# Both 512-token parts of a recurrence head in one step, turned outputs, advance splits of pooling maps, and wider tiles for branch A's gates: one decoder layer on Trainium2

## Chip, cores and metric

The kernel runs on one core of one Trainium2 chip. The metric is the device time of one execution, in microseconds (us); lower is better.

## The reference, cut to what matters

One layer of a decoder trunk for 1024 tokens of width 1024, all in float32:

```python
x = x + 0.5 * swiglu_1(rms(x))                        # D_FF = 2816
h = rms(x); proj = h @ w_in                           # 1024 x 6656, columns q, f, i, og, pool, gate A, gate B
# A: 8 heads, a state of 128 x 128 per head
f = lb + (1 - lb) * sigmoid(f)
S_t = diag(f_t) S_{t-1} + outer(1 - f_t, i_t)
o_t = S_t^T silu(q_t)                                 # RMS norm per head, times silu(og), then @ w_branch_a
# B: trailing means over 2, 4, 8, 16 tokens minus the token, a 128 x 128 map per group,
#    a scale per channel, then @ w_branch_b
y = sigmoid(gate_A) * y_A + sigmoid(gate_B) * y_B
x = x + y @ w_out
x = x + 0.5 * swiglu_2(rms(x))
x = x + sigmoid(rms(x) @ w_gate) * rms(p @ w_ple)
return rms(x)
```

## The kernel before

**Products.** Every big product is cut into 2 x 2 blocks and computed by a scheme of seven block products instead of eight (`SIDES`). Each float32 operand is split into a high part (ScalarE's cast, L118) and a low part (VectorE's subtraction, L119), and a product is three matmuls, high x high, high x low, low x high, of 128x128 by 128x512 (`mm3`, L157 to L159). Three such matmuls are called a triple here. `pair` computes two column blocks of a projection: it yields once per triple, 28 times (`PAIR`), and the last products are deferred into the next pair. Sums of weight blocks are GpSimd's (L90, L93).

**Stages.** The first feed-forward part runs from 0 to about 715 us. The projections by `w_in` and, between them, the recurrence run from about 775 to 1450. Then come the rest of branch B's product with `w_branch_b` (`branch_b`) and the loading of the recurrence's outputs (`load_act`), to 1485; branch A's product with `w_branch_a`, whose results are gated and added to branch B's (to about 1570); the product with `w_out`; the second feed-forward part; the embedding's gate; and the final norm, to 2415.

**The recurrence.** `hgrn(h, half)` computes one of the two 512-token halves of a head without a loop over tokens. Its tiles are `qk` (q and k side by side, 128x1024), `f`, `tot` (products of f over 2, 4, 8 ... tokens), `v` and `og`. The diagonal of the score matrix comes from a product of k and q (L925, copied under a mask at L927). Seven levels follow (`LEVELS`, hh = 1 to 64): four small matmuls (L954), float32 by float32, which are eight passes; then the copy of their result into the scores, under a mask on VectorE (L958) for hh < 32 and by ScalarE (L966) from 32 on; then one VectorE multiply of q and k by the products of f (L974, through the helper `mul`, L87), which the next level's matmuls read. After the levels k is transposed (L981, copied at L983), k times v (L986) gives the state updates (L998, L1000), and the scores and the state give the outputs (L1009, L1011). The norm follows: four squares on ScalarE (L1015), `rstd` on VectorE (L168) and GpSimd (L169), and a VectorE multiply (L1017). `turn` transposes the result (L1025), multiplies by the gate (L1026) and stores it. The transposes of `v` (L933) stand ahead of the levels.

**Order.** TensorE's order is as the program writes it (`tc.manual_schedule`). `hgrn` yields 13 times per half, and `head` runs half 0 and then half 1, 26 steps per head (`GROUPS`). At each step `among` puts some triples of the head's three `pair` generators behind the small matmuls: 84 triples per head, 74 in head 7, 4 more in heads 0 and 2 for the pooling maps. `turn` of a half is issued at step 2 of the next half, and the last one after the loop. For the other engines and for SyncE, which issues all DMAs (`load`, L149; `store`, L153), a scheduler sets the order at build time; each engine's queue is then worked through in order.

**Memory.** PSUM has three banks for `pA`, one each for `pB` and `pC`, and three for `aux`, which all small matmuls, transposes and pooling maps share. In SBUF a tile takes a buffer of its tag: "q" has four of 1024 columns, "h" five of 512, "w" twelve of 1024, "a" 28 of 1024, "u" eight of 512. `v`, `og`, `tot`, `ga` and `yb` use "h"; `qk` uses "q", and so do four of the `x` tiles of the product with `w_out`.

**Pooling maps.** `pool_maps` runs as one of the generators of heads 0 and 2: two groups by two halves, and for each a split (`hilo_half`, L118 and L119) followed at once by the triple that reads it, the scale and the store. The trailing means that a map reads are VectorE work spread beside an earlier pair (`beside_means`).

**Branch A.** For each of 32 results `done` loads 512 columns of `ga` and of `yb` into two "h" tiles, multiplies (L87), adds (L84) and stores.

Of the kernel before, what the change touches and what calls it, by code (L numbers as in the profile page):

```python
# [13 lines left out]
AF = mybir.ActivationFunctionType  # L14
# [23 lines left out]
def hybrid_block(ctx: ExitStack, tc: tile.TileContext, a: dict, out: bass.AP):  # L38
# [47 lines left out]
    def mul(o, x, y):  # L86
        nc.vector.tensor_tensor(o, x, y, ALU.mult)  # L87
# [672 lines left out]
    def qf_pair(h):  # L760
        qk, f = [t_("q", "qk") for _ in range(2)], [t_("u", "f") for _ in range(2)]
        heads[h] = qk, f

        def q_(half):
            def go(q):
                k = qk[half][:, R]
                nc.scalar.activation(k, q, AF.Sigmoid)
                mul(q, q, k)
            return go

        def f_(half):
            def go(src):
                nc.scalar.activation(f[half], src, AF.Sigmoid)
                nc.vector.tensor_scalar(
                    f[half], f[half], lb1[:, h : h + 1], lb[:, h : h + 1], ALU.mult, ALU.add
                )
            return go
# [87 lines left out]
    def pool_maps():  # L865

        r = t_("h", "pwr")
        load(r.rearrange("p (g d) -> p g d", g=NG), a["pool_w"].rearrange("g c d -> c g d"))
        wh, wl = hilo_half(r, "w", "pwhl")
        while pooled:  # L870
            g, u = pooled.pop(0)
            gc = slice(g * P, (g + 1) * P)
            for half in range(2):
                ph, pl = hilo_half(u[half], "w", "pb")
                ps = bank("aux")
                mm3(ps, wh[:, gc], wl[:, gc], ph, pl, True, True)
                nc.scalar.mul(u[half], ps, pscale[:, g : g + 1])
                store(m_dram[g][half], u[half])
                yield False
# [14 lines left out]
    v_next = []  # L894

    def v_load(h, half):
        assert (h, half) in v_there
        return load(t_("h", "v"), v_dram[h][half], True)

    def v_of(h, half):  # L900
        return v_next.pop() if v_next else v_load(h, half)


    states = {}

# [3 lines left out]
    def hgrn(h, half):  # L909
# [8 lines left out]
        state = states.get(h)  # L918
# [7 lines left out]
        yield  # L926
# [4 lines left out]
        ps = bank("aux")  # L931
        for p_, v_ in zip(chunks(ps), chunks(v)):
            nc.tensor.transpose(p_, v_, ident)  # L933
        yield
        nc.scalar.copy(v, ps)
        vc = chunks(v)
# [3 lines left out]
        at = 0  # L940
        for hh in LEVELS:
            n = HALF // (2 * hh)
            pv = tots[hh].rearrange("p (a two) -> p a two", two=2)
            tots[2 * hh] = tot[:, at : at + n]
            mul(tots[2 * hh], pv[:, :, 0], pv[:, :, 1])
            at += n
        mul(q, q, f)
        for hh in LEVELS:
# [6 lines left out]
            yield  # L955
# [15 lines left out]
            na = HALF // (2 * hh)  # L971
            both = view(qk, hh, [[HALF - hh, 2], [2 * hh, na], [1, hh]])
            by = view(tots[hh], 0, [[1, 2], [2, na], [0, hh]])
            mul(both, both, by)  # L974

        need = 4 - half
        ps = bank("aux")
        for p_, a_ in zip(chunks(ps)[:need], kc):  # L980
            nc.tensor.transpose(p_, a_, ident)  # L981
        yield
        nc.scalar.copy(k[:, : need * P], ps[:, : need * P])  # L983
# [3 lines left out]
        yield  # L987
        assert (h, half) in og_there
        og = load(t_("h", "og"), og_dram[h][half], True)
        og_last[0] = latest[0]  # L990
        befores = []

        for c, (s_, p_) in enumerate(zip(chunks(f), chunks(ps))):
# [5 lines left out]
            else:  # L999
                nc.vector.scalar_tensor_tensor(  # L1000
                    s_, state, tots[128][:, c : c + 1], p_, ALU.mult, ALU.add
                )
            state = s_
        states[h] = state

# [6 lines left out]
        yield  # L1012
# [19 lines left out]
    GROUPS = 2 * 13  # L1032
    turns = []

    def head(h):

        for half in range(2):
            for i, _ in enumerate(hgrn(h, half)):
                if i == 2 and turns:
                    turns.pop(0)()  # L1040
                if i == 7:
                    at = 2 * h + half + 1
                    if at < 2 * HEADS:
                        v_next.append(v_load(at // 2, at % 2))
                yield
# [342 lines left out]
```

## Time and profile before

| | us |
|---|---|
| median of 3 runs (2415.89 to 2421.88) | 2416.18 |
| the profiled execution | 2417.04 |
| its span in the trace | 2415.3 |
| TensorE matmul busy | 2330.6 |
| TensorE weight load busy (beside the matmuls) | 1916.1 |
| VectorE busy | 1471.4 |
| ScalarE busy | 980.0 |
| GpSimd busy | 444.8 |

The DMAs moved 331.75 MB, 137 GB/s over the span. In the rows of the profile PE is TensorE, PEld its weight loads, DVE VectorE, ACT ScalarE, POOL GpSimd, SP or SPq SyncE's queue. A row of the timeline has the start and the duration in us, the engine, the line of the kernel, the operation, the tile written and the tiles read (buffer numbers left out), and the shape; a bracket at its end says how long the engine idled just before it and for whom. A row of waits has the sum, the number and the longest, in us. A row of the stretches has the window and its length, then for PE, PEld, DVE, ACT and POOL the busy time and the number of instructions, then the granted TensorE clock, the share of time in which the DMA engines were busy, and GB/s; where the view was asked for one engine alone, only that engine's busy time stands there. A row of groups has busy time and mean ns of one, then the engine's idle time before them. Busy matmuls overlap a little in the trace, so a matmul's price is read from start to start.

### The profile page before, as it was taken

What the parts mean: (1) busy time and instruction counts of PE and PEld (TensorE: products, weight loads), DVE (VectorE), ACT (ScalarE), POOL (GpSimd) and SP (SyncE); (2) the same over time, 40 slices, a digit from 0 to 9 for tenths busy, and PEclk for the clock granted to TensorE, in tenths of its full rate; (3) what the DMA queues carried; (4) which work ended last, traced back from release to release, by engine and by line L of the source; (5) the groups of instructions that cost most, each with busy time, mean ns of one, the idle gap of its engine ahead of it and who ended that gap; (6) DMA issues with size and microseconds to landing.
All of it is one profiled execution on the core that took longest, in us unless ns stands there. A gap on an engine that the chain in (4) does not pass through costs nothing. (4 is left out here: it accounts for less than half of the span.)

```text
span 2415.3 us, 29471 instructions
## 1 busy us (share of the span) xinstructions
PE 2330.6 (96%) x11058; PEld 1916.1 (79%) x11058; DVE 1471.4 (61%) x2037; ACT 980.0 (41%) x1528; POOL 444.8 (18%) x397
## 2 busy tenths in 40 slices
PE   8999999999998999999999999999899999999997
PEld 6778888888877888788888877877687888888886
DVE  6555554567656766766566566676544544568568
ACT  6344333333554333333333343237333333334556
POOL 1332223200011222122222102102222222100000
PEclk9999999999999999999999999999999999999999
DMA  4344453484332232222222257652234533663334
GB/s 183 127 143 168 156 174 132 153 322 128 117 114 70 79 96 83 75 88 79 83 81 86 88 189 247 229 207 105 87 129 146 177 102 110 215 251 127 97 100 152
DMA packets 133759, 331.75 MB, mean 137 GB/s; under 512 B 15216, under 2 KB 16240, under 8 KB 133616
## 3 DMA queue, kind: packets, MB, share of 16 engines
q1 hardware_dynamic: 133616, 329.87, 40.1%
q8 instruction: 87, 1.43, 0.3%
q14 instruction: 56, 0.46, 0.1%
HBM read 228.62 MB, written 101.19 MB: 137 GB/s over the span
## 5 line engine op out<-in xcount | busy, mean ns | idle before, releaser
L90 POOL TENSOR_TENSOR s<-rb 128x512 f32<-128x512 f32 x74 | 98.5, 1331 | 780.1 <-DMA rb<-in_ffn_w_dram 352.6
L119 DVE TENSOR_TENSOR wtl<-rb,wth 128x1024 fp32r<-128x1024 f32 x74 | 90.7, 1225 | 152.7 <-ACT wth L118 152.7
L118 ACT CAST wsh<-s 128x1024 fp32r<-128x1024 f32 x74 | 77.8, 1052 | 229.6 <-POOL s L93 215.5
L119 DVE TENSOR_TENSOR wsl<-s,wsh 128x1024 fp32r<-128x1024 f32 x74 | 91.3, 1233 | 117.9 <-ACT wsh L118 117.9
L93 POOL TENSOR_TENSOR rb<-ra,s 128x512 f32<-128x512 f32 x74 | 96.7, 1306 | 349.0 <-DVE wd L119 335.6
L118 ACT CAST wth<-rb 128x1024 fp32r<-128x1024 f32 x74 | 77.7, 1049 | 183.8 <-POOL rb L93 183.8
L954 PEld LDWEIGHTS aux<-qk 128*128 128x128 f32 (+1 forms) x896 | 109.7, 186 | 37.9 <-issue 11.5
L118 ACT CAST gh<-gr 128x1024 fp32r<-128x1024 f32 x84 | 81.8, 980 | 141.8 <-PE aux L158 86.4
L119 DVE TENSOR_TENSOR wal<-ra,wah 128x1024 fp32r<-128x1024 f32 x74 | 91.5, 1238 | 75.1 <-PE pC L158 45.0
L119 DVE TENSOR_TENSOR gl<-gr,gh 128x1024 fp32r<-128x1024 f32 x84 | 95.0, 1134 | 68.2 <-ACT gh L118 68.1
L157 PE MATMUL pA<-xT3h,wth 128*128 128x512 f32 x296 | 119.7, 404 | 8.9 <-ACT g L382 6.8
L954 PE MATMUL aux<-qk 128*128 128x64 f32 (+1 forms) x896 | 110.5, 267 | 17.2 <-DVE qk L87 11.5
L118 ACT CAST wah<-ra 128x1024 fp32r<-128x1024 f32 x74 | 77.6, 1050 | 117.6 <-DMA ra<-in_ffn_w_dram 97.2
L157 PE MATMUL pA<-xT1h,wsh 128*128 128x512 f32 x280 | 114.1, 408 | 10.4 <-ACT xT1h L118 7.1
L157 PE MATMUL pB<-xT1h,wsh 128*128 128x512 f32 x296 | 119.3, 403 | 2.6 <-DVE g L81 1.3
L157 PE MATMUL pA<-x0h,wah 128*128 128x512 f32 x296 | 118.5, 400 | 1.2 <-DVE gb L87 0.7
L157 PE MATMUL pC<-x0h,wah 128*128 128x512 f32 x296 | 118.9, 402 | 0.0
L157 PE MATMUL pB<-x,wth 128*128 128x512 f32 x296 | 118.8, 401 | 0.0
L158 PE MATMUL pA<-x0l,wah 128*128 128x512 f32 x296 | 115.8, 391 | 1.6 <-DVE x0l L119 1.6
L158 PE MATMUL pB<-xT1l,wsh 128*128 128x512 f32 x296 | 116.6, 394 | 0.8 <-DVE xT1l L119 0.8
L157 PE MATMUL pA<-xT3h,wd 128*128 128x512 f32 x280 | 112.8, 403 | 4.3 <-ACT c L385 2.5
L159 PE MATMUL pA<-xT3h,wtl 128*128 128x512 f32 x296 | 116.4, 393 | 0.5 <-DVE wtl L119 0.5
(341 smaller groups left out, 6602.1 us busy)
## 6 DMA issues: line engine op xcount, KB each, us to landing
ra<-in_ffn_w_dram SPq DMA_DIRECT2D x47, 512.0 KB, 3.7
rb<-in_ffn_w_dram SPq DMA_DIRECT2D x44, 512.0 KB, 3.7
gsS<-gs SPq DMA_DIRECT2D x88, 256.0 KB, 2.2
rB<-in_ffn_w_dram SPq DMA_DIRECT2D x40, 512.0 KB, 7.0
gr<-gsS SPq DMA_DIRECT2D x40, 512.0 KB, 3.4
gsA<-g SPq DMA_DIRECT2D x66, 256.0 KB, 2.0
gr<-gsA SPq DMA_DIRECT2D x30, 512.0 KB, 5.9
ra<-in_w_in_dram SPq DMA_DIRECT2D x27, 512.0 KB, 3.6
```

Source lines behind the costliest of these rows:

```text
L90: nc.gpsimd.tensor_tensor(o, x, y, ALU.add)
L93: nc.gpsimd.tensor_tensor(o, x, y, ALU.subtract)
L118: nc.scalar.copy(hi, src)
L119: nc.vector.tensor_tensor(lo, src, hi.bitcast(F32), ALU.subtract)
L157: nc.tensor.matmul(ps, ah, bh, start=first, stop=False, **kw)
L158: nc.tensor.matmul(ps, ah, bl, start=False, stop=False, **kw)
L159: nc.tensor.matmul(ps, al, bh, start=False, stop=last, **kw)
L954: nc.tensor.matmul(ps[:m, c, :64], kc[c][:, :m], right, start=True, stop=True)
```

## The change

It has three parts. Lines of the changed kernel lie some lower: L928 is the product of k and q, L944 the level matmuls, L952 the masked copy, L960 ScalarE's copies, L975 the transposes of `v`, L984 those of k, L992 k times v, L1001 and L1003 the state updates, L1013 and L1015 the outputs, L1020 the norm's multiply, L1028 and L1029 the turn.

1. **Recurrence.** The two halves of a head run side by side: one step holds the same step of half 0 and of half 1, and a head has 12 steps instead of 26. In a level the multiply now stands ahead of the masked copy. The products of f are made one per level instead of all at the start; the last ones go into a constant tile (`decays`, in the room of `lbr`). k = 1 - f is made when q and f are finished (`k_` in `qf_pair`). `v` is loaded at the third level (hh = 4) and transposed after the last level; `og` is loaded at the step of the k transposes. A head's two turns are issued at steps 1 and 2 of the next head, and those of head 7 one behind the other after the loop.
2. **Pooling maps.** The split of the next map is issued one part ahead of the map that reads it, the first one in a part of its own, so heads 0 and 2 have 5 more parts instead of 4.
3. **Branch A.** `ga` and `yb` are loaded into the halves of one 1024-column "q" tile instead of two "h" tiles.

```diff
@@ qf_pair
+        def k_(half):
+            if half in made:
+                nc.scalar.activation(qk[half][:, R], f[half], AF.Copy, scale=-1.0, bias=1.0)
+            made.add(half)
...
@@ pool_maps
-        while pooled:
-            g, u = pooled.pop(0)
+        todo = [(g, half, u[half]) for g, u in pooled for half in range(2)]
+        pooled.clear()
+        parts = [hilo_half(todo[0][2], "w", "pb")]
+        yield False
+        for i, (g, half, u) in enumerate(todo):
             gc = slice(g * P, (g + 1) * P)
-            for half in range(2):
-                ph, pl = hilo_half(u[half], "w", "pb")
-                ps = bank("aux")
-                mm3(ps, wh[:, gc], wl[:, gc], ph, pl, True, True)
...
+            if i + 1 < len(todo):
+                parts.append(hilo_half(todo[i + 1][2], "w", "pb"))
+            ps = bank("aux")
+            mm3(ps, wh[:, gc], wl[:, gc], *parts.pop(0), True, True)
...
@@ hgrn
-        nc.scalar.activation(k, f, AF.Copy, scale=-1.0, bias=1.0)
-        v = v_of(h, half)
+        yield
...
-        for hh in LEVELS:
-            n = HALF // (2 * hh)
-            pv = tots[hh].rearrange("p (a two) -> p a two", two=2)
-            tots[2 * hh] = tot[:, at : at + n]
-            mul(tots[2 * hh], pv[:, :, 0], pv[:, :, 1])
-            at += n
-        mul(q, q, f)
...
         for hh in LEVELS:
+            yield
...
                 nc.tensor.matmul(ps[:m, c, :64], kc[c][:, :m], right, start=True, stop=True)
-            yield
+            na = HALF // (2 * hh)
+            both = view(qk, hh, [[HALF - hh, 2], [2 * hh, na], [1, hh]])
+            by = view(tots[hh], 0, [[1, 2], [2, na], [0, hh]])
+            mul(both, both, by)
             if hh < 32:
...
-            mul(both, both, by)
+            at = HALF - HALF // hh
+            pv = tots[hh].rearrange("p (a two) -> p a two", two=2)
+            tots[2 * hh] = decays[half] if hh == 64 else tot[:, at : at + na]
+            mul(tots[2 * hh], pv[:, :, 0], pv[:, :, 1])
+            if hh == 4:
+                v = load(t_("h", "v"), v_dram[h][half], True)
...
-    GROUPS = 2 * 13
+    GROUPS = 12
...
@@ head
-        for half in range(2):
-            for i, _ in enumerate(hgrn(h, half)):
-                if i == 2 and turns:
-                    turns.pop(0)()
...
-                yield
+        two = [hgrn(h, half) for half in range(2)]
+        for it in two:
+            next(it)
+        for i in range(GROUPS):
+            for it in two:
+                next(it, None)
+            if i in (1, 2) and turns:
+                turns.pop(0)()
+            yield
...
-            among(its, head(h), (74 if h == 7 else 3 * PAIR + 4 * (h in (0, 2))))
-        turns.pop(0)()
+            among(its, head(h), (74 if h == 7 else 3 * PAIR + 5 * (h in (0, 2))))
+        while turns:
+            turns.pop(0)()
...
@@ branch A, done
-            ga = load(t_("h", "ga"), ga_dram[j + i][half])
-            yb = load(t_("h", "yb"), yb_dram[j + i][half])
+            both = t_("q", "gy")
+            ga = load(both[:, L], ga_dram[j + i][half])
+            yb = load(both[:, R], yb_dram[j + i][half])
```

The first place is VectorE's queue in a head, from the masked copy of the level hh = 2 to the multiply of the level hh = 8 (before); `score_5481` is half 0's score matrix and `score_5482` half 1's, `o` tiles are results of projections, and `wsl` and `wtl` low parts of weights.

```order
L958 COPY_PREDICATED score_5481<-mask_77,aux_8696 128x128x2
L87 TENSOR_TENSOR qk_8188<-qk_8188,tot_8660 128x2x128x2
L87 TENSOR_TENSOR qk_8602<-qk_8602 128x512
L87 TENSOR_TENSOR o_8409<-o_8409,pA_8434 128x512
L958 COPY_PREDICATED score_5481<-mask_81,aux_8715 128x64x4
L87 TENSOR_TENSOR qk_8188<-qk_8188,tot_8660 128x2x64x4
L81 TENSOR_TENSOR o_8407<-o_8407,pB_8530 128x512
L119 TENSOR_TENSOR wsl_8823<-s_1591_8819,wsh_8822 128x1024
L87 TENSOR_TENSOR o_8407<-o_8407,sg_8730 128x512
L958 COPY_PREDICATED score_5481<-mask_85,aux_8740 128x32x8
L87 TENSOR_TENSOR qk_8188<-qk_8188,tot_8660 128x2x32x8
```

The same place after:

```order
L1029 SCALAR_TENSOR_TENSOR og_8454<-aux_8723,onorm,og_8454 128x512
L81 TENSOR_TENSOR o_8391<-o_8391,pB_8512 128x512
L119 TENSOR_TENSOR wsl_8835<-s_1593_8831,wsh_8834 128x1024
L87 TENSOR_TENSOR o_8391<-o_8391,sg_8737 128x512
L87 TENSOR_TENSOR qk_8200<-qk_8200,tot_8596 128x2x64x4
L952 COPY_PREDICATED score_5481<-mask_81,aux_8758 128x64x4
L87 TENSOR_TENSOR qk_8201<-qk_8201,tot_8604 128x2x64x4
L952 COPY_PREDICATED score_5482<-mask_81,aux_8768 128x64x4
L119 TENSOR_TENSOR wd_8838<-rb_8829,wd_8838 128x512
L119 TENSOR_TENSOR wtl_8844<-rb_8829,wth_8843 128x1024
```

Before, each level is a masked copy and then the multiply that the next level waits for, with projection work between levels. Now a level is two such couples, multiply first, one per half, with the projection work (`wd`, `wtl`) behind both.

The second place is the end of head 7 on VectorE, from the last state updates of half 1 to the last turn; `gb` rows are branch B's gates, `b` rows and `x0l` the sums and splits of the recurrence's earlier outputs in `load_act`.

```order
L1000 SCALAR_TENSOR_TENSOR f_9835<-f_9835,tot_10796,aux_10949 128x128 x2
L84 TENSOR_TENSOR b_1925_11170<-b_1926_11171,b_1925_11170 128x512
L168 TENSOR_SCALAR rso_11001<-rso_11001 128x4
L87 TENSOR_TENSOR gb_10964<-yb_10966,gb_10964 128x512
L1017 TENSOR_TENSOR qk_9833<-aux_10978,rso_11001 128x512
L84 TENSOR_TENSOR b_1926_11171<-b_1926_11171 128x512
L87 TENSOR_TENSOR gb_10995<-yb_10997,gb_10995 128x512
L1026 SCALAR_TENSOR_TENSOR og_10973<-aux_11020,onorm,og_10973 128x512
```

After, for both halves:

```order
L1003 SCALAR_TENSOR_TENSOR f_9838<-f_9838,lbr,aux_10925 128x128 x2
L168 TENSOR_SCALAR rso_10969<-rso_10969 128x4
L1020 TENSOR_TENSOR qk_9835<-aux_10961,rso_10969 128x512
L119 TENSOR_TENSOR x0l_11177<-b_1925_11170,x0h_11176 128x1024
L168 TENSOR_SCALAR rso_10986<-rso_10986 128x4
L84 TENSOR_TENSOR b_1925_11170<-b_1926_11171,b_1925_11170 128x512
L1020 TENSOR_TENSOR qk_9836<-aux_10977,rso_10986 128x512
L87 TENSOR_TENSOR gb_10996<-yb_10998,gb_10996 128x512
L1029 SCALAR_TENSOR_TENSOR og_10883<-aux_11013,onorm,og_10883 128x512
L1029 SCALAR_TENSOR_TENSOR og_10890<-aux_11020,onorm,og_10890 128x512
```

Before, only half 1's norm (L168, L1017) stands here. Now the norms of both halves do, with `x0l` and an addition between them. On TensorE 18 matmuls of `branch_b` lay between the last output matmul and the turn; now 12 lie between the last output matmul and the two turns.

The third place is SyncE's queue: loads of `x` for the product with `w_out` (rows with `x_dram`), before among branch B's stores.

```order
L149 DMA x_12141<-x_dram_9_136 128x1024
L153 DMA yb_dram_0_151_278<-gb_11303 128x512
L149 DMA ra_11515<-in_w_branch_a_dram 128x1024
L153 DMA yb_dram_1_152_279<-gb_11320 128x512
L153 DMA yb_dram_0_153_280<-gb_11342 128x512
L149 DMA x_12150<-x_dram_10_137 128x1024
L153 DMA yb_dram_1_154_281<-gb_11359 128x512
L149 DMA rb_11521<-in_w_branch_a_dram 128x1024
L149 DMA x_12159<-x_dram_11_138 128x1024
L149 DMA x_12168<-x_dram_12_139 128x1024
```

After, the same loads:

```order
L149 DMA y_11994<-y_dram_0_157_284 128x512
L149 DMA y_11994<-y_dram_0_161_288 128x512
L149 DMA x_12125<-x_dram_9_136 128x1024
L149 DMA rB_2069_12001<-in_w_out_dram 128x1024
L149 DMA rB_2072_12007<-in_w_out_dram 128x1024
L149 DMA rB_2075_12013<-in_w_out_dram 128x1024
L153 DMA y_dram_1_170_297<-o_11801 128x512
L153 DMA y_dram_0_169_296<-o_11802 128x512
L149 DMA y_12019<-y_dram_0_163_290 128x512
L149 DMA y_12019<-y_dram_0_167_294 128x512
L149 DMA x_12134<-x_dram_10_137 128x1024
L149 DMA x_12143<-x_dram_11_138 128x1024
```

They have moved behind branch A, to where the product with `w_out` fetches `y` and its weights.

More of the change, by code (lines that the diff above doesn't have):

```diff
@@ L892, in pool_pair @@
         yield from out_pair(w_in[PU + g], w_in[PU + g + 1], act, done)
[L894 to L901, printed above, removed]
     states = {}
+    decays = [lbr[:, i, :4] for i in range(2)]
     def view(t, offset, dims):
@@ L969, in hgrn @@
                     )
[L971 to L974 removed]
+            at = HALF - HALF // hh
[3 more added lines that the diff above has]
+            if hh == 4:
+                assert (h, half) in v_there
+                v = load(t_("h", "v"), v_dram[h][half], True)
+        yield
+        ps = bank("aux")
+        for p_, v_ in zip(chunks(ps), chunks(v)):
+            nc.tensor.transpose(p_, v_, ident)
+        nc.scalar.copy(v, ps)
+        vc = chunks(v)
         need = 4 - half
+        yield
         ps = bank("aux")
```

38 lines of the change are left out of this document (15 added, 23 removed).

## The prediction

> **What bounds the kernel now.** I read the page first, then the stretches, then PE's waits in the stretch that the change touches, and PE's timeline around each wait.
>
> ```profile
> PE 2330.6 (96%) x11058; PEld 1916.1 (79%) x11058; DVE 1471.4 (61%) x2037; ACT 980.0 (41%) x1528; POOL 444.8 (18%) x397
> 775.00:1450.00 675.00, 651.58 (x3579) 548.39 (x3578) 431.42 (x737) 248.84 (x496) 139.66 (x105) 0.98 0.29 94
> 1485.00:1570.00 85.00, 80.69 (x348) 64.47 (x347) 56.44 (x70) 25.10 (x32) 17.83 (x12) 1.00 0.66 216
> 1570.00:1600.00 30.00, 26.61 (x109) 21.17 (x108) 22.02 (x25) 10.05 (x10) 0.00 (x0) 0.94 0.93 346
> ```
>
> TensorE is the bound everywhere: 96% of the span, 651.6 of 675 us in the recurrence (775 to 1450), where VectorE works 431 us, 64%. So the change can only win what PE loses there: its waits, and the time after a wait in which its clock is low. The second and third stretches are branch A and the entry of the product with `w_out`. PE's waits in the recurrence:
>
> ```profile
> PE aux L954 <- DVE qk L87: 11.5, 13, 3.2
> PE aux L954 <- DVE tot L87: 4.2, 3, 1.4
> PE aux L933 <- DMA v<-v_dram: 2.5, 1, 2.5
> PE aux L158 <- DVE pb L119: 2.4, 1, 2.4
> ...
> PE aux L954 <- ACT pb L118: 0.8, 1, 0.8
> PE aux L954 <- ACT o L820: 0.6, 1, 0.6
> ```
>
> Read the first row so: matmuls of line 954 (one level of the recurrence) waited 13 times for the VectorE multiply that prepares the level, 11.5 us in all. All rows of L954 together: 17.1 us. What a wait costs beyond itself stands in PE's timeline (starts, durations, and in brackets the wait):
>
> ```profile
> 781.48 0.64 PE L933 MATMUL aux<-ident,v 128*128 128x128 f32 x4 [2.47 <-DMA v<-v_dram]
> ...
> 782.35 0.63 PE L158 MATMUL pC<-x0l,wah 128*128 128x512 f32 x1
> 782.78 0.63 PE L159 MATMUL pC<-x0h,wal 128*128 128x512 f32 x1
> ...
> 1166.56 1.08 PE L954 MATMUL aux<-qk 128*128 128x64 f32 x8 [1.37 <-DVE qk L87]
> ...
> 1413.89 1.94 PE L954 MATMUL aux<-qk 128*128 128x64 f32 x8 [3.23 <-DVE qk L87]
> 1415.59 0.77 PE L157 MATMUL pB<-x,wth 128*128 128x512 f32 x1
> ```
> ```profile
> 1004.60 0.79 PE L158 MATMUL aux<-pb,pwhl 128*128 128x512 f32 x1 [2.38 <-DVE pb L119]
> ...
> 1006.89 1.80 PE L954 MATMUL aux<-qk 128*128 128x64 f32 x8
> 1008.46 0.77 PE L157 MATMUL aux<-pb,pwhl 128*128 128x512 f32 x1
> ```
>
> After 781.48 the 512-column matmuls start 0.43 us apart (782.35, 782.78), against 0.23 at full speed (735.65, 735.88, quoted below): half the clock, for 8 matmuls, 8 x 0.20 = 1.6 us. The same 8 follow the wait of 1.37 us at 1166.56. After 1413.89, 9 matmuls run so (1.8 us), the group itself takes 1.70 us instead of 0.81 (+0.9) and the next one 0.3 more: 3.0 us. After 1004.60, 11 matmuls (2.2) and a group of 1.57 (+0.8): 3.0 us. The other waits show none.
>
> **The clock, row and rule.** The rows give half speed after waits of 1.37, 2.38, 2.47 and 3.23 us. The Trainium skill ("TensorE: Matmul & The Clock Gate", Part 1 and the closing table) has the array fall to half rate after an idle window of about 3.4 us, and advises against gaps over about 3 us. By that rule only the wait of 3.23 us would have a slow tail, and the sum below would be 3.2 us smaller, 12.7 instead of 15.9. The trace disagrees for the three shorter waits, so the rows stand.
>
> **Part 1: both halves in one step.** PE issues the same matmuls; only their grouping changes, 26 groups a head to 12, so I first price a group.
>
> ```profile
> 789.24 1.00 PE L954 MATMUL aux<-qk 128*128 128x64 f32 x8
> 790.05 0.48 PE L157 MATMUL pA<-xT3h,wd 128*128 128x512 f32 x1
> 790.36 0.39 PE L158 MATMUL pA<-xT3l,wd 128*128 128x512 f32 x1
> ```
> ```profile
> 733.63 1.95 PE L255 MATMUL tr<-diag,x 128*128 128x128 f32 x16
> 735.34 0.48 PE L157 MATMUL pB<-x,wth 128*128 128x512 f32 x1
> 735.65 0.40 PE L158 MATMUL pB<-x,wth 128*128 128x512 f32 x1
> 735.88 0.39 PE L159 MATMUL pB<-x,wtl 128*128 128x512 f32 x1
> ```
>
> Eight small fp32 passes (four matmuls) take 0.81 us, and the next big matmul starts 0.08 late (0.31 instead of 0.23): 0.89. Sixteen in a row take 1.71 and 0.08: 1.79, which is twice 0.89. Joining two groups is worth nothing on PE; I take 0, with 0.04 us for each of 96 steps, 4 us, either way.
>
> What it moves is the room between dependent steps. Before, a head's 84 big triples (0.69 us each) are spread over 26 steps: 84 / 26 x 0.69 = 2.2 us between the end of a level's group and the next level's. In that time VectorE must finish what it is at, then the copy under a mask, then the multiply:
>
> ```profile
> L87 DVE TENSOR_TENSOR qk<-qk,tot 128x512 f32<-128x512 f32 x96 | 79.4, 828 | 26.9 <-PE aux L954 26.7
> L958 DVE COPY_PREDICATED score<-mask,aux 128x256 f32<-128x256 uint16 x80 | 44.3, 554 | 58.2 <-PE aux L954 58.1
> L119 DVE TENSOR_TENSOR wtl<-rb,wth 128x1024 fp32r<-128x1024 f32 x23 | 28.2, 1225 | 35.2 <-ACT wth L118 35.2
> DVE wtl L119 <- ACT wth L118: 35.2, 23, 2.5
> ```
>
> 0.55 + 0.83 = 1.4 of the 2.2 us: 0.8 to spare. VectorE works in order, so one `wtl` (1.2 us, behind a wait of 1.5 on average and up to 2.5 for ScalarE) in front of the pair makes PE late; that is what the 17.1 us are. After, 84 / 12 = 7 triples, 4.8 us, lie between steps, and the multiply stands ahead of the copy. The first half has 4.8 + 0.9 (the other half's group) = 5.7 us for 0.83; the second must follow 0.83 + 0.55 and has about as long: 4 us to spare. `wd`, the wait and `wtl` together (0.7 + 2.5 + 1.2 = 4.4) just fit. So I take the L954 waits as gone, apart from two of 1.8 us together in front of head 2's maps (part 2): 17.1 - 1.8 = 15.3. With them go the slow tails at 1166.56 and 1413.89, 1.6 + 3.0. The wait for `v` goes with its tail, 2.5 + 1.6: the load is now issued at the third level and used five steps, some 33 us, later. Removed: 15.3 + 4.6 + 4.1 = 24.0 us.
>
> Given back inside: at the starts of heads 2, 4 and 6 all twelve `tot` products stand in VectorE's row between the first two levels, and the state updates, now seven in one step, are mixed with 1.2 us subtractions. By the spare time above this fits barely; I take 2 us (0 to 8, one missed step of about 1 us at each of eight heads).
>
> At the end of head 7 there is no next head to hide the last norm:
>
> ```profile
> 1438.68 1.22 DVE L119 TENSOR_TENSOR x0l<-b,x0h 128x1024 fp32r<-128x1024 f32 x1
> ...
> 1442.64 0.28 ACT L1015 ACTIVATE qk<-aux 128x128 f32<-128x128 f32 x1 [1.48 <-PE aux L1011]
> 1443.81 0.17 DVE L168 TENSOR_SCALAR rso<-rso 128x4 f32<-128x4 f32 x1
> 1444.06 1.01 POOL L169 TENSOR_TENSOR rso<-rso,mhalf 128x4 f32<-128x4 f32 x1 [41.95 <-DVE rso L168]
> 1445.10 0.69 DVE L1017 TENSOR_TENSOR qk<-aux,rso 128x512 f32<-128x512 f32 x1 [0.38 <-POOL rso L169]
> ```
>
> The chain from the squares to the finished multiply takes 1445.79 - 1442.64 = 3.15 us, and 3.5 from the last matmul. Before, 18 big matmuls (4.1 us) cover it. Now 12 (2.8 us) stand between, and in VectorE's row an `x0l` of 1.2 and one subtraction come between the halves: half 1 is ready about 3.5 + 1.2 + 0.9 = 5.6 us after the group, and PE is at its turn after 2.8 + 0.4. I take a wait of 2.5 and a slow tail of 1.6: 4.1 us (0 to 7).
>
> Behind each added wait stand only the 15 remaining `yb` triples and branch A, which no one else delays.
>
> **Part 2: a map split in advance.** The wait of 2.4 us at 1004.60 is the first of head 2's four maps, and no later map waits. VectorE is what is late there:
>
> ```profile
> 984.00:1004.60 20.60, 19.10 (x49) 0.98 0.19 60
> ```
>
> In the 20.6 us before the map VectorE is busy 19.1 (the row is VectorE's alone): it computes the trailing means that the map reads. The advance split cannot start before the mean is there, and the new order keeps the same means and four multiplies of the levels in front of it. So nothing is won: 2.4 + 3.0 stay, and the 1.8 us of the two earlier waits move into it. From -5.4 (all gone) to +3. The splits themselves are the same instructions; in head 0, with shorter windows, they are hidden as now.
>
> **Part 3: the gates in large tiles.** Same loads, same multiplies; 85 - 80.69 = 4.3 us is all PE loses in branch A and its entry, mostly on other things. I take 0 (-2 to +2). But the tiles come from the four 1024-wide buffers that the next stage's `x` uses, so SP issues four loads later:
>
> ```profile
> 1477.07 0.38 SPq L149 DMA_DIRECT2D x<-x_dram  x1
> 1487.60 0.32 SPq L149 DMA_DIRECT2D x<-x_dram  x1
> 1497.40 2.55 SPq L149 DMA_DIRECT2D x<-x_dram  x2
> 1593.48 0.50 PE L157 MATMUL pC<-woh,yh 128*128 128x512 f32 x1 [3.14 <-ACT yh L118]
> ```
>
> Now they stand among the loads of `y` and `w_out`, which fall where the DMA is busy 0.93 of the time at 346 GB/s. 2.1 MB more take 2.1 / 0.346 = 6 us there; the first can go before 1570, where the share is 0.66. PE already waits 3.1 us at 1593.48 for `y`. I take +2 us (0 to 6).
>
> **Sum.** -24.0 + 2 + 4.1 + 0 + 0 + 2 = -15.9 us. The profiled execution took 2417.04 us, so 2401.1; it lies 0.9 above the median of the runs, 2416.18. For the median: 2400.
>
> **Rivals.** (a) VectorE's row still decides: where it stands 4 us behind its step, the doubled room is used up. For: `wd` and `wtl` fit with little over; twelve `tot` products at three heads. Against: 64% busy. If each of 8 heads keeps 1.5 us and the tail costs 7, it is -24 + 12 + 7 + 2 = -3 us: 2413. (b) Slower, by the banks: a step takes two of three `aux` banks, so the next step's second group needs the bank that VectorE's copy for this step's first half must empty. VectorE's work per step is 0.64 x 6.6 = 4.2 us; if waits add more than 2.4, PE waits for the copy in every step. At 0.4 us for 96 steps, 38 us, against the 16 won: +22, 2438. Against: the longest wait for `wth` is 2.5 and comes three times in a head, not every step. (c) The map's wait goes too and the banks cost nothing: 5.4 + 2 + 2 more, 2391.
>
> **Chances.** Forecast 0.60, (c) 0.10, (a) 0.19, (b) 0.11. The forecast's own range by its bounds is 2390 to 2408. To leave out no more than 2 in 10 it reaches to (c) and over half of (a): 2389 to 2413. A measurement of this kernel tells 0.3%, 7.2 us, from no change: the forecast, (c) and little of (a) are beyond it, so faster 0.72, same 0.18, slower 0.10.
>
> **What would show it.** Right: waits of the level matmuls (now L944) under 4 us in all, no wait for `v_dram`; a map wait of 2 to 5 us in head 2 with half speed behind it; one wait at L1028 at the end; `x` loads issued after 1555. Wrong: level waits of over 8 us, or waits of many steps for the masked copies; a step's 16 passes taking over 1.9 us; over 5 us at the first matmuls of the `w_out` product.

## The result, and the profile after

The changed kernel took 2390.36 us (median of 4 runs, 2388.05 to 2397.24) against 2417.64 us for the kernel before in the same comparison: a ratio of 0.9897, 95% interval 0.9881 to 0.9913. That is 27 us faster, 11 us more than the 16 of the forecast. The profiled execution took 2388.05 us.

First the page's line of busy times, then the same stretch of work in both kernels, from the first product of k and q in head 0 to the end of head 7's last turn (columns as in the stretches of the prediction; the first row is of the kernel before, the second of the changed one):

```profile
PE 2317.3 (97%) x11058; PEld 1916.3 (80%) x11058; DVE 1444.3 (61%) x2037; ACT 980.1 (41%) x1528; POOL 440.3 (18%) x397
```
```profile
775.23:1446.92 671.69, 648.27 (x3565) 545.67 (x3564) 428.18 (x732) 248.67 (x496) 139.66 (x105) 0.98 0.29 93
```
```profile
775.01:1414.53 639.52, 630.65 (x3565) 543.24 (x3564) 402.38 (x730) 247.34 (x494) 138.05 (x105) 0.99 0.30 97
```

The same 3565 matmul records take 639.52 us instead of 671.69: the recurrence gained 32.2 us. The span fell by only 29.0 (2415.3 to 2386.3); the rest of the kernel, from the turn to the end, takes 2386.3 - 1414.53 = 971.8 us against 968.4 before, so 3.4 us were given back. PE's waits between 775 and 1450 us in the changed kernel (sum, number, longest):

```profile
PE aux L158 <- DVE pb L119: 2.9, 1, 2.9
PE aux L1028 <- DVE qk L1020: 2.1, 1, 2.1
PE pA L157 <- ACT o L385: 1.2, 1, 1.2
PE aux L157 <- ACT pb L118: 1.2, 1, 1.2
PE pA L157 <- ACT wah L118: 0.9, 1, 0.9
PE pA L159 <- DVE wal L119: 0.5, 1, 0.5
```

The list is whole. No level matmul (L944) waits at all, where L954 waited 17.1 us before; the wait for `v` is gone; the map's wait in head 2 and a wait at the turn (L1028) remain, as forecast. One sign of the forecast missed: the four moved loads of `x` go out between 1532.38 and 1549.66 us, not after 1555. Heads 1 and 3 to 6, the ones without a map and before the last, now take the same time each. Head 3 before, and then in the changed kernel, from its first product of k and q to the next head's (timeline, start and duration):

```profile
1035.61 1.05 PE L925 MATMUL aux<-qk 128*128 128x128 f32 x8
1117.28 1.05 PE L925 MATMUL aux<-qk 128*128 128x128 f32 x8
```
```profile
1024.97 1.95 PE L928 MATMUL aux<-qk 128*128 128x128 f32 x16
1103.61 1.95 PE L928 MATMUL aux<-qk 128*128 128x128 f32 x16
```

81.67 us have become 78.64. But the kernel before had only two level waits in this head, 1.7 us in all. So something besides the bracketed waits was won, and that, with the 3.4 us given back, is what the experiments had to find.

### The profile page after: what moved, and what is told of

It reads as the page before. It is cut to its first block, busy times and chain, and to the rows that moved or that the text cites. A ratio compares the mean times of both kernels' runs of the same rounds, so it can differ in the third digit from the quotient of the medians.

```text
span 2386.3 us, 29429 instructions
## 1 busy us (share of the span) xinstructions
PE 2317.3 (97%) x11058; PEld 1916.3 (80%) x11058; DVE 1444.3 (61%) x2037; ACT 980.1 (41%) x1528; POOL 440.3 (18%) x397
## 4 chain that ended last, share of the span: by engine, by line
PE 72%; DVE 9%; DMA 7%; ACT 4%; POOL 4%; issue 3%; SPq 1%; POOLq 0%; DVEq 0%; ACTq 0%
PE pA L157 11%; PE pA L159 11%; PE pA L158 11%; PE pB L157 5%; PE pB L159 5%; PE pB L158 5%; PE aux L944 4%; PE pC L159 3%; PE pC L157 3%; PE pC L158 3%; PE aux L158 3%; PE aux L159 3%; PE aux L157 3%; DMA rb<-in_ffn_w_dram 2%; POOL s L93 1%
## 5 line engine op out<-in xcount | busy, mean ns | idle before, releaser
L93 POOL TENSOR_TENSOR rb<-ra,s 128x512 f32<-128x512 f32 x74 | 95.9, 1295 | 317.0 <-DVE wd L119 302.5
L118 ACT CAST wah<-ra 128x1024 fp32r<-128x1024 f32 x74 | 77.7, 1051 | 129.9 <-DMA ra<-in_ffn_w_dram 87.5
L159 PE MATMUL pA<-x0h,wal 128*128 128x512 f32 x296 | 116.1, 392 | 0.5 <-DVE wal L119 0.5
L158 PE MATMUL pA<-xT3l,wth 128*128 128x512 f32 x296 | 116.5, 394 | 0.0
L159 PE MATMUL pB<-xT1h,wsl 128*128 128x512 f32 x296 | 116.5, 393 | 0.0
```

The source lines that it names most:

```text
L93: nc.gpsimd.tensor_tensor(o, x, y, ALU.subtract)
L118: nc.scalar.copy(hi, src)
L158: nc.tensor.matmul(ps, ah, bl, start=False, stop=False, **kw)
L159: nc.tensor.matmul(ps, al, bh, start=False, stop=last, **kw)
```

## The experiments

Each ratio is to the kernel before, measured in the same comparison. "The changed kernel" below is the one with all three parts.

### Which part did it

**Parts 1 and 2, gates as before.**

```diff
-            both = t_("q", "gy")
-            ga = load(both[:, L], ga_dram[j + i][half])
-            yb = load(both[:, R], yb_dram[j + i][half])
+            ga = load(t_("h", "ga"), ga_dram[j + i][half])
+            yb = load(t_("h", "yb"), yb_dram[j + i][half])
```

> The changed kernel with the gates' loads put back into two 512-column tiles (part 3 undone). The changed kernel took 2390.4 us and loses about 7 us more than before between the start of branch A and the product with w_out (its lead of 32.9 us over before shrinks to 25.3), of which the entry gives 2.3 back. Theory: the wide gate tiles cause it, since they share the four q buffers with the tiles that the recurrence's outputs are loaded into. Then this kernel gains 4 to 7 us: 2383 to 2386, without the waits of 1.66 us at the first product of branch A and of 1.82 us at VectorE's addition. Rival: the new end of the recurrence (both turns last) puts ScalarE and VectorE late for branch A; then it stays at 2389 to 2393 and the waits stay.

2389.68 us, 0.9889 (0.9876 to 0.9903): no different from the changed kernel. The wait at branch A's first product is still 1.25 us and the one for VectorE's addition is 3.51. The theory that the gate tiles make branch A late fell; the rival, the new end of the recurrence, stood.

**Part 1 alone**: the same, with `pool_maps` and its count of parts as before.

> Part 1 alone on the kernel before: the two halves side by side, pooling maps and gate tiles as before. If the advance splits are worth nothing, it equals the run without the wide gate tiles within 2 us, and the wait of the first map in head 2 stays between 2 and 4 us. Rival: the split in advance is what keeps the later maps from waiting now that steps are twice as long; then this kernel is 3 to 8 us slower than that run, with waits at line 158 in more than one map.

2388.79 us, 0.9882 (0.9867 to 0.9897). The first map waits 2.94 us, as in the changed kernel. Part 1 is the whole gain.

**Part 2 alone**: the changed kernel's `pool_maps` and its count of parts in the kernel before.

> Part 2 alone on the kernel before. By the prediction 0, between -5.4 and +3 us: 2412 to 2420, the wait of the first map in head 2 at 2 to 5 us. Rival: the split goes ahead and the wait with its slow tail goes: 2411 to 2412.

2417.62 us, 1.0008 (0.9998 to 1.0018), and the map's wait is 2.4 us, as before. Worth nothing. VectorE's timeline of the changed kernel says why:

```profile
991.47 2.49 DVE L119 TENSOR_TENSOR pb<-o,pb 128x512 fp32r<-128x512 f32 x4
```
```profile
974.80:991.40 16.60, 15.98 (x43) 0.97 0.23 64
```

All four splits run one behind the other (x4). In the 16.6 us ahead of them VectorE is busy 16.0 (second row, VectorE alone): the means come as late as they did, so a split issued ahead has nothing to start on.

**Part 3 alone**: the wide gate tiles in the kernel before.

> Part 3 alone on the kernel before. By the theory that the wide gate tiles make branch A late: 4 to 7 us slower than before, 2421 to 2425, with new waits of PE in the first 60 us of branch A. By the prediction's step, +2 us (0 to 6), at the first product with w_out and not in branch A. By the rival (the recurrence's end is the cause): 0, or 1 to 2 us faster, since the wait at the entry of the product with w_out shrinks.

2413.23 us, 0.9987 (0.9978 to 0.9997): if anything a little faster, and branch A has no new wait. The part that the prediction charged with 2 us, for the later loads of `x`, helped: PE's wait for `yh` at the entry of the product with `w_out` is 1.8 us instead of 3.1, here and in the changed kernel, and 3.1 again in the three kernels above without part 3. That it is the place of those loads is argued, not shown.

### Distance, order, or the joining of groups

**Masked copy first in the changed kernel.**

```diff
...
-            mul(both, both, by)
             if hh < 32:
...
+            mul(both, both, by)
```

> The changed kernel with the masked copy ahead of the multiply in each level again, everything else as changed. Theory (the doubled distance between dependent steps is what ended the waits): each multiply is ready 0.55 us later in a spare of about 4 us, so level waits stay under 1 us in all, plain heads keep 78.6 us and the time stays at 2389 to 2392. Rival (the order multiply first did it): level waits of 4 to 9 us return and the time is 2395 or more.

The recurrence did as the theory said: no level wait, and four of the five heads without a map and before the last take 78.64 us, the fifth 79.03. The time was 2395.28 us, 0.9901 (0.9886 to 0.9916), outside the 2389 to 2392 that was expected and where the rival had put it, but the interval covers the changed kernel's ratio and the rival's level waits are absent. What the trace shows lost stands behind the recurrence: a new wait of 2.11 us at 1510.43, and one more stretch at half the clock, from 1592.19. Once the distance is doubled, the order in a level matters nothing. The trace also shows the distance at work: from starts and modelled ends, 16 of the 80 multiplies by `tot` that a next level reads end more than 2.2 us behind their own level's group, which is the room that the kernel before had, and still each ends at least 2.5 us before the next level's group starts.

**Multiply first in the kernel before**, with its 26 steps.

```diff
+            na = HALF // (2 * hh)
+            both = view(qk, hh, [[HALF - hh, 2], [2 * hh, na], [1, hh]])
+            by = view(tots[hh], 0, [[1, 2], [2, na], [0, hh]])
+            mul(both, both, by)
             if hh < 32:
...
-            mul(both, both, by)
```

> The kernel before with one edit: the multiply ahead of the masked copy in each level, 26 steps a head as before. Theory (distance decides): each of the 18 level waits shrinks by at most one copy, 0.55 us, so of 17.1 us some 8 to 11 stay, and the time is 2405 to 2412. Rival (the order did it): the level waits fall under 3 us and the time is 2397 to 2402, most of the change's gain from this edit alone.

2403.49 us, 0.9939 (0.9924 to 0.9954). PE's largest waits between 775 and 1450 us:

```profile
PE aux L954 <- DVE qk L87: 5.3, 7, 1.1
PE aux L158 <- DVE pb L119: 3.5, 1, 3.5
PE aux L933 <- DMA v<-v_dram: 2.2, 1, 2.2
PE aux L954 <- ACT o L820: 1.7, 1, 1.7
```

Level waits of 7.0 us stay, 10.1 are gone; the longest for the multiply fell from 3.2 to 1.1. Both lie between the theory (8 to 11 us stay, 2405 to 2412) and the rival (under 3, 2397 to 2402). So four moved lines bring some 15 us of the 27: order and distance cure the same waits, the order in part, the longer step wholly, and their gains don't add. Part 1 also makes the products of f level by level and k ahead; no run has these without the longer step or the step without these, so their share stays open. The prediction had taken them together and could not have said so.

**Two groups a step**: the changed kernel with the big triples spread between half 0's and half 1's group.

```diff
-    GROUPS = 12
+    GROUPS = 24
...
             for it in two:
                 next(it, None)
-            if i in (1, 2) and turns:
-                turns.pop(0)()
-            yield
+                if it is two[1] and i in (1, 2) and turns:
+                    turns.pop(0)()
+                yield
```

> The changed kernel with each step cut into two, half 0's group and half 1's group apart with the big triples spread between: 24 groups a head, and the same distance between dependent steps. It prices the grouping alone. By the prediction's row (two groups of 0.89 us against one of 1.79) a plain head stays at 78.6 us, but for the last level, whose 8 passes took 0.61 us and whose 16 take 1.08: 0.1 to 0.4 us more a head, 1 to 3 us in all, 2391 to 2394. Rival (joining is worth what is missing in the sum, some 9 us over 8 heads): plain heads at 79.7 to 80.0 us and 2398 to 2401.

2386.03 us, 0.9869 (0.9849 to 0.9889): less than either expected, mainly because this kernel loses nothing in branch A (below). In the recurrence the price is plain. Head 4, from its first group to the next head's:

```profile
1103.31 1.05 PE L928 MATMUL aux<-qk 128*128 128x128 f32 x8
...
1150.50 0.68 PE L944 MATMUL aux<-qk 128*64 128x64 f32 x8
...
1182.75 1.05 PE L928 MATMUL aux<-qk 128*128 128x128 f32 x8
```

79.44 us against 78.64 for the joined groups: 0.80 a head, and an estimated 6.4 us over eight. It is between theory (0.1 to 0.4) and rival (1.1 to 1.4). Some 0.36 of it is the last level: a group of 8 takes 0.61 us from start to start and 16 take 1.08, and each group costs some 0.2 us more at its two boundaries, where matmuls start 0.33 us apart instead of 0.23. The rest, 0.44, is 0.04 us for each of the other 11 joined groups, which was the prediction's bound and not its value.

### Where 7.3 us went in branch A

In the changed kernel branch A starts 32.9 us earlier than before (1453.06 against 1485.98), but the product with `w_out` starts only 25.7 us earlier (its first matmul into `pC` at 1547.66 against 1573.32): 7.3 us are lost (7.6 in the expectations, which read another matmul). SyncE's queue shows what is late: the raw weights of branch A's second pair. Second `ra` and branch A's first matmul, before and then in the changed kernel:

```profile
1482.92 0.33 SPq L149 DMA_DIRECT2D ra<-in_w_branch_a_dram  x1
```
```profile
1485.98 0.47 PE L157 MATMUL pA<-x0h,wah 128*128 128x512 f32 x1 [0.68 <-DVE gb L87]
```
```profile
1459.27 0.38 SPq L149 DMA_DIRECT2D ra<-in_w_branch_a_dram  x1
```
```profile
1453.06 0.47 PE L157 MATMUL pA<-x0h,wah 128*128 128x512 f32 x1 [0.18 <-DVE gb L87]
...
1457.02 0.51 PE L157 MATMUL pA<-x0h,wah 128*128 128x512 f32 x1 [1.66 <-ACT x0h L118]
...
1507.89 0.50 PE L157 MATMUL pB<-xT1h,wsh 128*128 128x512 f32 x1 [1.82 <-DVE o L81]
```

Before, the load went out 3.1 us ahead of branch A; now it goes out 6.2 us behind. It is the sign of a whole queue that is late, and not itself the cause of the first wait: that wait ends at 1457.02, before the load goes out. The first pair's `ra` is late too, 16.1 us ahead of branch A instead of 21.4, and ScalarE has `x0h` right behind a split that waited for GpSimd's sum of those weights:

```profile
1454.98 1.05 ACT L118 CAST wth<-rb 128x1024 fp32r<-128x1024 f32 x1 [3.41 <-POOL rb L93]
1455.93 1.04 ACT L118 CAST x0h<-b 128x1024 fp32r<-128x1024 f32 x1
```

The splits of later pairs are late in the same way, and PE waits again in the middle of branch A. From start to start, 2.7 of the 7.3 us are longer waits, 2.7 are matmuls at half the clock behind the waits of 1.66 and 1.82 us, and the rest is short gaps and slower starts that have no bracket.

**Outputs loaded through other buffers.** `load_act` loads the recurrence's outputs in four steps of two 1024-wide tiles; all came from the four "q" buffers, of which head 7's two halves hold one each, now both until the turns.

```diff
-        b1, b2 = t_("q", "b1"), t_("q", "b2")
+        b1, b2 = (t_("w" if i in (0, 1) else "q", s) for s in ("b1", "b2"))
```

> The changed kernel with one edit in the loading of the recurrence's outputs: the first two of four steps take their two tiles from the 12 w buffers instead of the four q buffers. Theory: with both halves of head 7 in flight their q tiles come free only at the two turns, so the outputs are loaded 5 to 6 us later against branch A's start than before, and behind them in SyncE's queue the weights of branch A; that is the 7.6 us lost in branch A. Then with the other tiles the second raw weight of branch A is issued before or at branch A's start (before: 3.1 us ahead, changed: 6.2 us behind), the waits of 1.66 and 1.82 us with their slow tails go, and the time is 2383 to 2387. Rival (the loss comes from something else at the end of the recurrence, and the order on the queue is only its sign): 2388 to 2392 with these waits still there.

2384.26 us, 0.9860 (0.9845 to 0.9874). The second `ra` is back at 3.1 us ahead of branch A, and branch A loses nothing (87.6 us against 87.3). But head 7 takes 79.0 us instead of 75.0: six output loads now go out in one bunch, ScalarE waits 4.6 us for the first of them, and PE waits for ScalarE behind it:

```profile
1397.14 0.50 PE L157 MATMUL pA<-xT3h,wd 128*128 128x512 f32 x1 [3.33 <-ACT o L385]
```

**The first and the third step instead**: the same line with `i in (0, 2)`.

> The changed kernel with the first and the third step of loading the outputs taken from the w buffers (in the run before it the first and the second were). The lead over before at branch A's end was then kept (28.9 to 29.6 us), but head 7 lost 4 us to a wait of 3.33 us for ScalarE, behind a bunch of six output loads. Here the loads of two steps are not bunched in front of head 7's end. Theory (buffers set when the outputs are loaded): head 7 back to 74 to 76 us, and branch A's loss under 3 us instead of 7.6: 2381 to 2385. Rival (what branch A gains head 7 pays, since ScalarE does the splits of the outputs in either place): 2384 to 2388 with head 7 at 78 us or more.

2379.54 us, 0.9853 (0.9837 to 0.9868): below both ranges, the fastest of all, and below the changed kernel's interval. The second `ra` goes out 3.1 us ahead again, no wait in branch A exceeds 0.8 us, and head 7 takes 77.6 us: 2.6 of what branch A gains are paid in head 7.

**The last turns later.**

```diff
+        late = branch_b(1)
+        for _ in range(4):
+            next(late)
         while turns:
             turns.pop(0)()
+        steps(late)
...
     for j in range(1, KC):
-        steps(branch_b(j))
+        if j > 1:
+            steps(branch_b(j))
```

> The changed kernel with four more triples of branch B (2.8 us) ahead of the two last turns. The wait at L1028 was 2.09 us and had no slow tail. By the norm's chain (half 1 ready about 5 us behind the last output matmul) the wait goes: 2.1 us less at this place. In SyncE's queue the second raw weight of branch A then stands ahead of one of the last stores instead of behind all of them; if its place decides branch A's loss, one to three us more come back there: 2384 to 2388. Rival (the outputs leave later, so branch A starts with the same wait): the wait at L1028 goes and comes back at branch A's first product: 2389 to 2392.

2388.07 us, 0.9884 (0.9868 to 0.9900). The wait at L1028 went, and waits of 1.0 (twice), 1.67 and 1.54 us stand around branch A's start: the rival, by the trace; the time tells neither.

**Both**: the first and third step from "w", and the later turns.

> The two edits that each helped, together: two of the output loading steps from the w buffers, and four more triples of branch B ahead of the last two turns. The first alone took 2379.5 us with a wait of 1.72 us left at L1028; the second alone took that wait away. If they add, 2376 to 2379. If the triples moved ahead of the turns only shift the wait (branch A's first product waits for the last outputs instead), it stays at 2379 to 2382.

2382.32 us, 0.9857 (0.9836 to 0.9879): they don't add, and the time is no better than that of the first fix alone.

Over all these kernels the time of branch A goes with the place of that one load, the mark of how late the queue is. Issue of the second `ra` after branch A's start, and the time from there to the first product with `w_out` into `pC`:

| kernel | second `ra`, us | branch A, us |
|---|---|---|
| before | -3.1 | 87.3 |
| part 2 alone | -3.6 | 86.3 |
| multiply first | -3.4 | 88.3 |
| part 3 alone | -3.1 | 87.2 |
| outputs, steps 0 and 1 | -3.1 | 87.6 |
| outputs, steps 0 and 2 | -3.1 | 86.3 |
| both fixes | -3.1 | 89.8 |
| two groups a step | -1.3 | 87.5 |
| late turns | 1.5 | 89.6 |
| part 1 alone | 5.6 | 94.5 |
| parts 1 and 2 | 5.7 | 91.8 |
| copy first | 6.1 | 95.7 |
| changed kernel | 6.2 | 94.6 |
| means on GpSimd | 6.2 | 95.9 |

That the buffers of the loaded outputs decide it in the changed kernel is shown by the one-line edits; they bring the outputs and the weights forward together, so which of the two PE lacked is not separated. That half 0's earlier turn does it where a step has two groups is only argued. The 89.8 of both fixes has another cause: two waits of 0.75 us for the weights of `w_out`, and half the clock behind them.

### The map's wait

**Half of the means on GpSimd.**

```diff
-                add(n[:, sh:], c[:, sh:], c[:, :-sh])
+                (pool_add if half else add)(n[:, sh:], c[:, sh:], c[:, :-sh])
```

> The changed kernel with the trailing means' additions of the second half on GpSimd (14 of them, 7 per group) instead of VectorE. Theory (VectorE is what is late for the maps of head 2): about 7 x 0.68 = 4.8 us of VectorE's work ahead of the maps goes, and the waits of 1.19 and 2.94 us with the slow tail of 1.6 us shrink to under 2 us in all: head 2 at 84 to 87 us instead of 90.6, 2384 to 2387. Rival (GpSimd's additions, about 1.3 us each, are late in turn, or the maps wait for the means' last step, not for VectorE's total): head 2 stays at 89 us or more, 2389 to 2395.

2389.98 us, 0.9893 (0.9872 to 0.9915), head 2 at 89.9 us, the map's wait 3.6: the rival. VectorE has fewer additions, but what is left takes longer beside GpSimd's (see the last section). The wait of head 2 stays open as a thing to win.

## Why the prediction was right, and where it missed

The forecast (2400 us, range 2389 to 2413) had the sign, the part and the mechanism: VectorE's lateness within a level, ended by the longer distance. Its size was 11 us short. In the profiled executions:

- **Level waits** (taken as 15.3 of 17.1, with slow tails of 4.6). All of them went, and they were worth more than their brackets. The wait that the trace gives as 1.42 us in head 3:

```profile
1054.49 0.40 PE L159 MATMUL pA<-xT1h,wsl 128*128 128x512 f32 x1
1056.31 1.08 PE L954 MATMUL aux<-qk 128*128 128x64 f32 x8 [1.42 <-DVE tot L87]
1057.19 0.48 PE L157 MATMUL pB<-xT1h,wsh 128*128 128x512 f32 x1
```

  Without it the group would have started 0.23 us behind the matmul, at 1054.72; it started 1.59 later, and ran 0.88 us instead of 0.81. So the wait cost 1.66: 0.24 more than its bracket, which counts from the modelled end of the matmul. All 18 level waits start 0.16 us later than their brackets say, and 17 of their groups run 0.88 to 0.92 us (the last runs at half the clock). At 0.24 each that is 4.3 us. This step's term was mis-sized: it summed brackets.
- **Joining groups** (0, with 4 us either way). Mis-sized too: 6.4 us. The working compared the price of 8 wide passes with that of 16, which holds (0.81 and 1.70 us), and left out the last level, whose passes are narrower, and kept as a bound what the other 11 joined groups do save, 0.04 us each.
- **Head starts** (+2): nothing. Heads 4 to 6 take 78.64 us each, whatever stands at their start.
- **The tail** (a wait of 2.5 and a slow tail of 1.6): the wait is 2.1, the tail did not come.
- **Part 2** (0): right, and for the reason given; the map still waits, 2.9 us, with half the clock behind it, and two more waits of 1.2 and 0.9 us stand beside it. Head 2 gained nothing: 90.55 us against 90.21, so the maps took back what its levels and groups gave.
- **Part 3** (0, and +2 for the loads of `x`): 0 was right; the 2 had the wrong sign.
- **What the sum lacked**: branch A, 7.3 us lost, of which 1.9 come back within the product with `w_out`, most of it by the shorter wait at its entry (1.8 us instead of 3.1). The prediction said that behind the tail stands "branch A, which no one else delays". It had counted the waits behind the last turn, not the buffers that both halves hold until it.

Together: the recurrence gave 32.2 where 17.9 was forecast. Of the 14.3 us between, the groups are 6.4, the brackets 4.3, the head starts 2.0 and the tail 2.0, 14.7 in all; the 1.8 us of level waits that the forecast let move into the map's wait did so, as head 2 shows. These are estimates, good to about a microsecond. Later stages took 3.4 where 2 was forecast.

That the time lies inside the range is in part luck. It is at the edge even of the forecast's own range (2390 to 2408), and the loss in branch A, which no term of the sum held, kept it there: the two kernels that load the outputs through other buffers and have no such loss take 2384.26 and 2379.54 us, outside 2389 to 2413.

One sum of the prediction is off: if waits under 3 us had no slow tail, the 1.6 us at the last turn would go too, and the working in its paragraph on the clock would give 14.3 us instead of 12.7.

Of the rivals, (a), VectorE's order still deciding, and (b), the `aux` banks, have no wait in the list above. (c), the time nearest to the result, needed the map's wait to go; it did not. That the result lies at its 2391 us is no support for it. The single wait for `v` was not tried alone; only its absence is seen.

## What to carry to other kernels

Where a step on one engine must follow a step on another, work out how much other work lies between the two: with that distance doubled every level wait ended, reordering the engine's queue alone ended 10.1 of 17.1 us, and the second edit is four lines. Price a wait from start to start, not by its bracket. When two pieces of work run side by side, ask which buffers both now hold to the end, and what is queued behind the loads that wait for them.

## What the hardware showed that was not expected

**The same wait, with and without a slow tail.** One place in the first feed-forward part, untouched by the change, waits 2.46 us in both kernels. Before, and then in the changed kernel:

```profile
154.62 0.50 PE L157 MATMUL pA<-xT3h,wth 128*128 128x512 f32 x1 [2.46 <-ACT g L382]
154.95 0.39 PE L158 MATMUL pA<-xT3l,wth 128*128 128x512 f32 x1
155.18 0.40 PE L159 MATMUL pA<-xT3h,wtl 128*128 128x512 f32 x1
```
```profile
154.04 0.64 PE L157 MATMUL pA<-xT3h,wth 128*128 128x512 f32 x1 [2.46 <-ACT g L382]
154.48 0.63 PE L158 MATMUL pA<-xT3l,wth 128*128 128x512 f32 x1
154.91 0.63 PE L159 MATMUL pA<-xT3h,wtl 128*128 128x512 f32 x1
```

The first goes on 0.23 us apart, the second 0.43 for 3.4 us. With parts 1 and 2 alone even a wait of 3.51 us had no slow tail:

```profile
1505.14 0.50 PE L157 MATMUL pB<-xT1h,wsh 128*128 128x512 f32 x1 [3.51 <-DVE o L81]
1505.47 0.40 PE L158 MATMUL pB<-xT1l,wsh 128*128 128x512 f32 x1
1505.71 0.39 PE L159 MATMUL pB<-xT1h,wsl 128*128 128x512 f32 x1
```

In the kernel before, one of 1.37 had one. The granted clock shows what differs. In each trace it changes only at marks a multiple of 3.413 us apart, and where the marks fall differs from trace to trace. The two windows between marks that hold the wait of 2.46 us, before and then in the changed kernel (window, length, PE's busy time alone, clock, DMA):

```profile
150.50:153.91 3.41, 1.65 (x8) 1.00 0.41 154
153.91:157.33 3.42, 2.71 (x12) 1.00 0.16 59
```
```profile
150.83:154.24 3.41, 0.95 (x5) 1.00 0.27 100
154.25:157.66 3.41, 3.41 (x9) 0.50 0.43 160
```

Before, a mark cuts the wait: PE idles 1.76 us in one window and 0.71 in the next. In the changed kernel the whole wait lies in one window, and the next one runs at half the clock. A mark cuts the wait of 3.51 us too, into 1.76 and 1.75. Take all 14 traces and add up PE's gaps of over 0.15 us in each window at full clock ahead of the one with PE's last matmul: all 73 windows with over 1.92 us of them were followed by one at half the clock, 30 of the 103 with 1.36 to 1.92 us were, and none with less. Waits in one window add up: 1.19 us and the first 1.24 of the next wait, together 2.43, stand ahead of the slow stretch at 990.51 in the changed kernel. So a slow tail of some 1.6 us hangs on where the marks fall, which a sum cannot know; it should carry the tail as a chance. The Trainium skill ("TensorE: Matmul & The Clock Gate", Part 1) says that the window of about 3.4 us over which activity is judged runs freely; the marks here agree with that, but a whole idle window, which the page asks for, was not needed here.

**VectorE's small copies held by GpSimd.** With the means on GpSimd, first VectorE's copies and then GpSimd's additions at the same time:

```profile
985.17 0.14 DVE L857 COPY pw<-o 128x1 f32<-128x1 f32 x1
...
985.95 1.00 DVE L857 COPY pw<-pw 128x2 f32<-128x2 f32 x1
...
987.60 1.00 DVE L857 COPY pw<-pw 128x4 f32<-128x4 f32 x1
```
```profile
985.52 1.41 POOL L90 TENSOR_TENSOR pw<-pw 128x510 f32<-128x510 f32 x1 [3.54 <-DVE pw L81]
987.47 1.10 POOL L90 TENSOR_TENSOR pw<-pw 128x508 f32<-128x508 f32 x1 [0.54 <-DVE pw L81]
```

Copies of two and four columns, 0.16 us in the changed kernel, take 1.00 and end within 0.03 us of GpSimd's addition. The Trainium skill ("SBUF — State Buffer", SBUF: two separate sides) calls the port pair that the two engines share an exclusive lock, held for a whole instruction; these rows agree. Work moved from VectorE to GpSimd was so in part paid for by VectorE: from half 0's addition of 511 columns to the first split for a map, in head 2, pass 16.4 us (975.30 to 991.74) against 17.3 in the changed kernel (974.22 to 991.47).
